# A hybrid diffusion layer on one core: the first stage rebuilt, with array turns over loaded tiles, splits on VectorE, and four jobs moved into it

## The chip, the cores and the metric

The kernel runs on one core of one Trainium2 chip. The metric is the device time of one execution in microseconds (us), lower being better; the figure of record is the median over the runs.

## The reference

One layer of a diffusion backbone over 512 latent tokens `x` (width 1024) with a prefix of 256 context tokens `ctx`, all in float32. A conditioning row `c` gives six modulation vectors of 1024 for the latent tokens (`silu(c) @ w_ada + b_ada`), a vector `c_ctx` gives them for the context:

```
hx = rmsnorm(x, g_pre_mix)   * (1 + scale)     + shift
hc = rmsnorm(ctx, g_pre_mix) * (1 + scale_ctx) + shift_ctx
px, pc = hx @ w_in, hc @ w_in          # cut into the inputs of three branches and three gates
a = HGRN2 recurrence, both directions, 4 heads of 128   (from a state over the context)
b = grouped-query attention over context and latent tokens, q and k normed, rotary
c = Hyena: dwconv3, u = v * x1, long convolution of u with filters, times x0
y = (sum of sigmoid(gate) * (branch @ w_o)) @ w_out
x = x + gate1 * rmsnorm(y);   x = x + gate2 * rmsnorm(ConvFFN(modulate(x)))
```

The Hyena filters come from a small network over 512 positions: three layers `h = sin(freq * (h @ w + b))` of width 64 (33 inputs), and a last matrix.

## The kernel before, in words

**Dense matmuls.** Activations are held transposed, channels on partitions, tokens along the row. Every large matmul is made of three passes of 32-bit operands that are split into a high and a low part: high weights by high activations, high by low, low by high (`passes`, matmul at L251). A split is a ScalarE copy that rounds (L206) and a subtraction that makes the remainder (L209), on VectorE unless the caller names GpSimd. `weights` issues the load of a weight tile into one of three buffers `w_raw` on SP's queue and splits it. A "job" is 8 k tiles x 3 passes = 24 matmuls of 512 columns with one weight tile; `stream` runs jobs in turn and loads `ahead` of them. L254 is the line of transposes.

**The first stage, `begin`.** It loads the tokens (`xT`, eight tiles of 128 x 512) and the first modulation tiles, and adds up the squares of the tokens (L527). A modulation vector isn't a matmul: for each of 128 x 1024 tiles of `w_ada` one VectorE instruction (L462, with its read of the accumulator) multiplies by the row `silu(c)`, which a matmul with ones has spread over all partitions, and sums along the row. `rstd_` makes the reciprocal root mean squares of the tokens: tiny matmuls of the squares with ones, VectorE's mean (L849), GpSimd's power (L850), four diagonal tiles (L853), and matmuls with ones that spread them (`rb`). Then, for each of the eight k tiles: the load of two modulation tiles and of one tile of `w_first` (six weight groups of 128, the heads' q and gate of heads 0 to 2), their split with the remainder on GpSimd, two modulation columns (L462, bias L490, scale L491), x times `rb` (L548), scale and shift on ScalarE, and the split into `hx_h` and `hx_l`. With each tile 18 matmuls run, six groups that stay open in PSUM banks 0 to 5 over all k tiles. At four of the tiles one step of the filter network (`filter_net`, `sin`, L326 to L333) stands between. Behind this the context is normed (`norm`, on GpSimd and VectorE), and six Hyena jobs run (`hy_jobs`, part 2 and 1 of channel tiles 0 to 2), with GpSimd making the weights' remainders. Each job ends in `conv3`: a ScalarE step (L865) and two VectorE steps (L866, L867) of a convolution of three taps. Between the steps of these jobs the context is modulated tile by tile into `hc`.

**The rest, `run`.** A planner (`weave`) walks through twelve streams in one fixed order of preference (the recurrence's mixes, states, outputs, the Hyena convolution, attention, the norms, and the dense jobs as the last) with assumed delays, and so fixes TensorE's order for good; where a stream of higher rank waits, a job fills. The jobs are taken in a list: heads 0 and 1 (two gate jobs and one of values each), two jobs of head 3, two Hyena jobs, head 2, and so on. A gate job has two matmul chains, one of 512 columns for the latent tokens and one of 256 for the context; each is evacuated by two sigmoids on ScalarE (L615, L616). The dense jobs alternate between two PSUM banks (`dbanks`). The other four modulation vectors are made behind numbered jobs (`ADA_AT`): each such job lets `ada_rest` issue one load (L586) and do one column (L462); the tiles of these loads lie in two buffers in turn.

**Engines run in order.** Each engine takes its instructions in the order of the program, and SP issues the loads, in order as well, each when the buffer it fills is free. ScalarE loads a table (ACT_TABLE_LOAD) when the next function is of another set.

## Time and profile before

| | |
|---|---|
| Runs | 1156.64, 1156.71 and 1157.84 us; median 1156.71 |
| Profiled execution | 1156.59 us, span of its trace 1154.8 us |
| TensorE busy | 1082.2 us (94%), 5746 matmuls |
| VectorE, ScalarE, GpSimd busy | 776.0, 500.4, 180.5 us |
| Mean granted clock of TensorE | 0.979 |
| Bytes moved | 119.70 MB, 104 GB/s over the span |
| First 131 us | TensorE 98.90 us busy, VectorE 112.20, GpSimd 48.69, 186 GB/s |
| 131 to 300 us | TensorE 168.83 us of 169 busy |

The trace is that of one execution. Times in it count from the start of its span; the execution lasts 1.8 us longer than the span. A row of the timeline has the start, the duration from the first to the last of the instructions it groups, the engine, the line, the operation, output and inputs by the program's names, shapes and number; in brackets stands the idle time ahead of it with what ended it. "PE" is TensorE, "DVE" VectorE, "ACT" ScalarE, "POOL" GpSimd, "SP" the engine that issues most loads. A row of stretches has for each engine the busy time and the number of instructions, and then the clock granted to TensorE, the share of the time in which the DMA engines were busy, and GB/s.

### The profile page before, as it was taken

Reading aid. Unit: us, or ns where it says so; the run is one execution under the profiler, and the core shown is the slowest. Engines: PE = TensorE matmul, PEld = TensorE weight load, DVE = VectorE, ACT = ScalarE, POOL = GpSimd, SP = SyncE. Lnnn points to the kernel's source line nnn. Section 1 sums busy time; section 2 is a strip of 40 time slices with the busy share of each in tenths; the row PEclk is TensorE's granted clock in tenths of the full one; section 3 lists DMA queues with packets and bytes.
Section 4 is the critical chain, followed back from the end, with each engine's and each line's share of the span. In section 5 each row is a group of like instructions: output and inputs, shape, how many; then the busy total and the mean of one; then the engine's idle time right before and its main releaser. Section 6 shows DMA issues by size and latency. Waiting matters only on the chain.

```text
span 1154.8 us, 14924 instructions
## 1 busy us (share of the span) xinstructions
PE 1082.2 (94%) x5746; PEld 922.5 (80%) x5746; DVE 776.0 (67%) x1265; ACT 500.4 (43%) x799; POOL 180.5 (16%) x179
## 2 busy tenths in 40 slices
PE   4888999999999988999999999889999999999995
PEld 2566799898888876977888878889888888888885
DVE  5998997968874775886667658365786666531124
ACT  4454543334333432665555555345444444332220
POOL 2256212011212022102111100320000000001112
PEclk9989999999998998999999999989999999999998
DMA  9632623513433211420112254111362332223212
GB/s 329 232 94 87 205 92 91 165 55 110 128 101 101 83 55 53 130 94 34 55 56 63 82 167 151 50 37 56 128 200 92 100 120 91 82 69 100 82 51 74
DMA packets 36437, 119.70 MB, mean 104 GB/s; under 512 B 3948, under 2 KB 6188, under 8 KB 36366
## 3 DMA queue, kind: packets, MB, share of 16 engines
q1 hardware_dynamic: 33980, 111.97, 29.9%
q0 software_dynamic: 1152, 4.19, 1.3%
q10 hardware_dynamic: 1234, 2.58, 0.7%
q8 instruction: 45, 0.74, 0.3%
q14 instruction: 26, 0.21, 0.1%
HBM read 116.63 MB, written 2.10 MB: 103 GB/s over the span
## 4 chain that ended last, share of the span: by engine, by line
PE 74%; DVE 14%; ACT 4%; issue 3%; POOL 2%; DMA 2%; ACTq 0%; DVEq 0%; POOLq 0%
PE banks L251 71%; DVE page L209 2%; PE banks L254 2%; DVE page L462 2%; ACT page L206 1%; DVE page L1362 1%; DVE page L1363 1%; DVE hx_l L209 1%; DMA page<-in_w_ada 1%; DMA w_raw<-in_w_in 1%; POOL page L853 1%; DVE wide L774 0%; POOL page L209 0%; DVE page L1071 0%; DVE wide L772 0%
## 5 line engine op out<-in xcount | busy, mean ns | idle before, releaser
L251 PE MATMUL banks<-hx_h,page 128*128 128x512 f32 (+1 forms) x1768 | 564.9, 389 | 16.7 <-ACT hx_h L206 4.5
L251 PEld LDWEIGHTS banks<-hx_h,page 128*128 128x128 f32 x1768 | 333.6, 192 | 85.9 <-issue 8.3
L251 PE MATMUL banks<-page,page 128*128 128x256 f32 (+4 forms) x1991 | 379.9, 323 | 10.5 <-ACT page L1254 5.5
L251 PE MATMUL banks<-hx_l,page 128*128 128x512 f32 (+1 forms) x872 | 338.3, 388 | 2.7 <-DVE hx_l L209 2.7
L251 PEld LDWEIGHTS banks<-page,page 128*128 128x128 f32 (+2 forms) x1991 | 303.2, 192 | 44.7 <-ACT page L1254 5.9
L209 DVE TENSOR_TENSOR page<-w_raw,page 128x1024 fp32r<-128x1024 f32 (+2 forms) x139 | 164.2, 1184 | 154.9 <-ACT page L206 99.7
L206 ACT ACTIVATE page<-w_raw 128x1024 fp32r<-128x1024 f32 (+2 forms) x154 | 155.9, 1016 | 140.0 <-PE banks L251 120.7
L251 PEld LDWEIGHTS banks<-hx_l,page 128*128 128x128 f32 x872 | 167.8, 192 | 32.5 <-DVE hx_l L209 3.6
L251 PE MATMUL banks<-thin,page 128*128 128x512 f32 (+1 forms) x367 | 112.9, 355 | 0.6 <-DVE thin L209 0.6
L251 PEld LDWEIGHTS banks<-thin,page 128*128 128x128 f32 x367 | 67.7, 191 | 9.8 <-DVE thin L209 1.1
L462 DVE SCALAR_TENSOR_TENSOR page<-page,page 128x1024 f32<-128x1024 f32 x52 | 63.4, 1221 | 7.4 <-DMA page<-in_w_ada 5.2
L1352 POOL TENSOR_TENSOR page<-page,thin 128x256 f32<-128x256 f32 x7 | 7.8, 1120 | 326.3 <-ACT thin L1302 326.3
L1172 POOL TENSOR_SCALAR page<-page,page 128x768 f32<-128x768 f32 x32 | 29.2, 914 | 169.7 <-DVE page L1171 166.0
L1170 ACT ACTIVATE page<-banks,page 128x768 f32<-128x768 f32 x32 | 31.7, 991 | 31.8 <-DVE page L1169 29.6
L206 ACT ACTIVATE page<-page 128x512 fp32r<-128x512 f32 (+1 forms) x45 | 24.7, 552 | 43.2 <-DVE page L1455 20.1
L254 PE MATMUL banks<-const,page 128*128 128x128 f32 x254 | 38.0, 275 | 1.1 <-ACT page L1031 1.1
L209 POOL TENSOR_TENSOR page<-w_raw,page 128x768 fp32r<-128x768 f32 (+1 forms) x14 | 32.4, 2312 | 42.0 <-ACT page L206 42.0
L254 PEld LDWEIGHTS banks<-const,page 128*128 128x128 f32 x254 | 31.8, 146 | 8.2 <-ACT page L1031 1.3
L206 ACT ACTIVATE page<-banks 128x512 fp32r<-128x512 f32 x41 | 24.1, 593 | 29.4 <-PE banks L254 29.4
L865 ACT ACTIVATE page<-banks,vec 128x512 f32<-128x512 f32 x40 | 30.5, 766 | 14.1 <-PE banks L251 14.0
L251 PEld LDWEIGHTS banks<-const,page 128*128 128x128 f32 x132 | 20.0, 219 | 17.5 <-DVE page L1407 7.5
L768 ACT ACTIVATE page<-wide 128x512 f32<-128x512 f32 x28 | 19.0, 678 | 34.1 <-DVE wide L774 18.0
(277 smaller groups left out, 1127.9 us busy)
## 6 DMA issues: line engine op xcount, KB each, us to landing
w_raw<-in_w_in SPq DMA_DIRECT2D x58, 512.0 KB, 3.5
w_raw<-in_w_up SPq DMA_DIRECT2D x44, 512.0 KB, 3.5
page<-in_w_ada SPq DMA_DIRECT2D x42, 512.0 KB, 4.4
w_raw<-in_w_down SPq DMA_DIRECT2D x16, 512.0 KB, 3.5
w_raw<-in_w_out SPq DMA_DIRECT2D x8, 512.0 KB, 3.8
w_raw<-in_w_first SPq DMA_DIRECT2D x8, 384.0 KB, 7.3
wide<-in_w_ada SPq DMA_DIRECT2D x6, 512.0 KB, 4.6
w_raw<-in_w_down SPq DMA_DIRECT2D x8, 384.0 KB, 3.1
```

The costliest lines, as they stand in the source:

```text
L206: self.nc.scalar.activation(h, x, AF.Copy, scale=1.0 if scale is None else scale)
L209: e.tensor_tensor(l, x, hf, op=SUB)
L251: self.on_pe(self.nc.tensor.matmul(out, w, x, start=start, stop=stop), max(n, 64) * (1 if x.dtype == F32R else 4))
L254: self.on_pe(self.nc.tensor.transpose(out, x, self.cv(C_ID, 128)), 256)
L462: self.nc.vector.scalar_tensor_tensor(junk, w, 1.0, row, op0=MUL, op1=MUL, accum_out=out)
L768: nc.scalar.activation(km.v(0, [(2 * b, n2), (b, 2), (1, b)]), kq.v(1024, [(2 * b, n2), (b - 1024, 2), (1, b)]), AF.Copy)
L853: (engine or nc.gpsimd).tensor_scalar(dg[:, c * 128:(c + 1) * 128], self.cv(C_ID, 128), ms[:, 4 + c:5 + c], 1.0, op0=MUL, op1=MUL)
L865: nc.scalar.activation(out, ps, AF.Identity, bias=w[:, 3:4], scale=w[:, 1:2])
L1170: nc.scalar.activation(p[:], s, AF.Exp, bias=st[:, 1:2], scale=r, accum_out=st[:, 2:3])
L1172: gp.tensor_scalar(p[:], p[:], st[:, 3:4], 1.0, op0=MUL, op1=MUL)
L1362: e.tensor_tensor(y, y, rs.v(0, [(0, 2), (1, 256)]), op=MUL)
L1363: e.tensor_tensor(r, r, y, op=ADD)
```

## The change

- **Start.** The tokens' loads alternate between SP's queue and ScalarE's; the constants' load comes behind them. Ones that the matmuls need come from a memset. The conditioning row is spread and passed through SiLU ahead of the squares. Behind each square, and over the first two pairs of modulation tiles, `warm` runs matmuls of ones with the loaded tile; nobody reads their bank. The tokens' `rb` comes from a function `shares`, whose diagonal is one instruction.
- **Splits** of `w_first` and of the Hyena weights: VectorE in place of GpSimd.
- **Modulation in three steps** (`modulated`): VectorE multiplies x by scale and `rb`, ScalarE adds the shift and rounds into `hx_h`, VectorE adds the shift and subtracts `hx_h`. The biases of two columns are added by one instruction (`mods_of`, now L494, L495).
- **Filter network folded**: the 512 positions lie as two halves of 256 on partitions 0 and 64, with block-diagonal weights. Its first layer stands ahead of the k tiles, the other two behind the dense jobs of `begin`; the last sine writes both halves into rows of 64.
- **Context later**: its row is made behind the k tiles, its squares after eight steps of the dense jobs, and its `rb` by `shares`; `norm` is gone.
- **Four jobs moved**: the q and gate jobs of head 3 and the two Hyena jobs of channel tile 3 go from the list of `run` into `begin`, which then runs ten dense jobs over five banks in turn. The second part of `ADA_AT` is four numbers lower.

Lines in the changed program stand a little apart: the split's L206 and L209 are L205 and L208, the gate's L615 and L616 are L639 and L640, `conv3` is L889 to L891, and the modulation's remainder is L484.

```diff
-ADA_AT = list(range(1, 28)) + list(range(90, 107, 2))
+ADA_AT = list(range(1, 28)) + list(range(86, 103, 2))
...
-NET = (1, 3, 5, 7)
...
-    def filter_net(self):
+    def filter_net(self, banks):
+
 
         nc, i = self.nc, self.i
-        sm, z = self.A(512), self.A(512)
-        nc.sync.dma_start(sm[:64, :196], i["hy_small"])
-        nc.sync.dma_start(z[:33, :], i["zT"])
-
-        h = None
-        arg, tmp = self.A(512), self.A(512)
+        n = T // 2
+        sm, z = self.A(512), self.A(n)
+        nc.scalar.dma_start(sm[:, :388], i["hy_small"])
+        nc.scalar.dma_start(z[:], i["zT"])
+
+        h, (arg, tmp) = z, (self.A(n) for _ in range(2))
         for l in range(3):
-            yield 9.0
-            ps = self.cbank()
...
+            yield
+            ps = self.bank(banks[l])[:, :n]
+            self.mm(ps, sm[:, 128 * l:128 * l + 128], h[:], True, True)
+            nc.vector.tensor_scalar(arg[:], ps, sm[:, 384 + l:385 + l], sm[:, 387:388], op0=ADD, op1=MUL)
+            self.sin(arg[:], tmp[:])
+            self.free(h)
+            if l < 2:
+                h = self.A(n)
+                nc.scalar.activation(h[:], arg[:], AF.Sin)
+        h = self.A(T)
+        for half in range(2):
+            nc.scalar.activation(h[:64, half * n:half * n + n], arg[64 * half:64 * half + 64, :], AF.Sin)
+        self.free(sm, arg, tmp)
         self.fh = h
...
-    def norm(self, xt, n):
+    def shares(self, ps, n, rb):
 
         nc, v = self.nc, self.nc.vector
...
+        k = n // 128
+        ms, dg = self.A(16), self.A(n)
+        v.tensor_scalar(ms[:, 0:k], ps.v(0, [(2, k)]), 1.0 / D, EPS, op0=MUL, op1=ADD)
+        nc.gpsimd.tensor_tensor(ms[:, 4:4 + k], ms[:, 0:k], self.cv(C_NH, k), op=ALU.pow)
+        v.tensor_tensor(dg.v(0, [(128, k), (1, 128)]), Buf(self.const).v(C_ID, [(0, k), (1, 128)]), ms.v(4, [(1, k), (0, 128)]), op=MUL)
+        for c in range(k):
+            self.mm(rb[:, c * 128:(c + 1) * 128], self.cv(C_ONE, 128), dg[:, c * 128:(c + 1) * 128], True, True)
+        self.free(ms, dg)
+
+    def modulated(self, m, o, ft, x, rb, hl):
+
+        nc, v = self.nc, self.nc.vector
+        n = x.shape[-1]
+        u, (h, l) = self.A(n), hl
+        shift = m[:, o + ft:o + ft + 1]
+        v.scalar_tensor_tensor(u[:, :n], x, m[:, o + 16 + ft:o + 17 + ft], rb, op0=MUL, op1=MUL)
+        self.last_mod = nc.scalar.activation(h, u[:, :n], AF.Identity, bias=shift).ins
+        v.scalar_tensor_tensor(l, u[:, :n], shift, h.bitcast(F32), op0=ADD, op1=SUB)
+        self.free(u)
+
+    def mods_of(self, m, o, ft, w, row, junk=None):
 
         v = self.nc.vector
         for part in range(2):
...
+            c = o + 8 * part + ft
+            self.ada(m[:, c:c + 1], w[part][:], row, w[part][:] if junk is None else junk)
+        p = m.v(o + ft, [(8, 2)])
+        v.tensor_tensor(p, p, Buf(self.vec).v(V_BADA + ft, [(8, 2)]), op=ADD)
+        v.scalar_tensor_tensor(m[:, o + 16 + ft:o + 17 + ft], m[:, o + 8 + ft:o + 9 + ft], 1.0, self.vv(V_G + ft), op0=ADD, op1=MUL)
 
     def begin(self):
 
         nc, i, v = self.nc, self.i, self.nc.vector
...
+        row, ones = self.A(1024), self.A(256)
+        v.memset(ones[:], 1.0)
         xb, cb = [self.A(512) for _ in range(8)], [self.A(512) for _ in range(4)]
         xt = [b[:] for b in xb]
...
         for k, b in enumerate(xb):
-            nc.sync.dma_start(b[:], i["xT"][:, k * 512:(k + 1) * 512])
-        rows = [self.A(1024) for _ in range(2)]
+            (nc.sync, nc.scalar)[k % 2].dma_start(b[:], i["xT"][:, k * 512:(k + 1) * 512])
+        nc.scalar.dma_start(self.const, i["const"])
+        net = self.filter_net((4, 5, 5))
+        next(net)
         self.row = rows[0]
         wada, groups = [], [Buf(self.bank(g)) for g in range(6)]
         def load_ada(ft):
...
+        load_ada(1)
+        for k in range(2):
+            ps = self.bank(k)
+            self.mm(ps, ones[0:1, :128], row[0:1, k * 512:(k + 1) * 512], True, True)
+            nc.scalar.activation(rows[0][:, k * 512:(k + 1) * 512], ps, AF.Silu)
+        self.free(row)
+        junk = self.A(1024)
+
+        def warm(x):
+            self.mm(self.bank(3), ones[:, :128], x, True, True)
         sqs = []
         for k in range(KT):
             sq = self.A(512)
-            last = nc.scalar.activation(sq[:], xt[k], AF.Square).ins
+            nc.scalar.activation(sq[:], xt[k], AF.Square)
+            warm(xt[k])
...
-        rs = self.rstd([sqs[0]], C_ONE, 1.0 / D, engine=v)
+        ps, rb = Buf(self.bank(7)), Buf(self.bank(6))
+        for c in range(4):
+            self.mm(ps[:, 2 * c:2 * c + 2], sqs[0][:, c * 128:(c + 1) * 128], ones[:, :2], c == 0, c == 3)
         self.free(sqs)
-        self.cbanks.remove(6 + self.comp_bank % 2)
-        net = self.filter_net()
+        self.shares(ps, T, rb)
+        for e in range(8):
+            warm(wada[e // 4][e // 2 % 2][:, e % 2 * 512:e % 2 * 512 + 512])
+        next(net)
         for ft in range(KT):
-            if ft:
+            if ft > 1:
                 load_ada(ft)
-            if ft in NET:
-                next(net, None)
-            wh, wl = self.weights(i["w_first"][ft], (6, 128), nc.gpsimd)
-            self.mods_of(m, ft, [b[:] for b in wada[ft]], rows[0][:], junk[:])
-            v.tensor_tensor(xt[ft], xt[ft], rs[:], op=MUL)
-            self.modulated(m, ft, xt[ft], self.hx[ft], "hx")
+            wh, wl = self.weights(i["w_first"][ft], (6, 128))
+            self.mods_of(m, 0, ft, wada[ft], rows[0][:], junk[:])
+            self.modulated(m, 0, ft, xt[ft], rb[:], self.hx[ft])
             for g in range(6):
                 s = slice(g * 128, (g + 1) * 128)
                 self.passes(groups[g][:], wh[:, s], wl[:, s], *self.hx[ft], ft == 0, ft == KT - 1)
             self.done((wh, wl))
+        self.free(xb, junk, ones)
+        rows.append(self.A(1024))
+        nc.sync.dma_start(rows[1][:], i["cond"][1:2, :].to_broadcast([128, D]))
+        nc.scalar.activation(rows[1][:], rows[1][:], AF.Silu)
         for k, b in enumerate(cb):
             nc.sync.dma_start(b[:], i["cT"][:, k * 512:(k + 1) * 512])
-        nc.sync.dma_start(rows[1][:], i["cond"][1:2, :].to_broadcast([128, D]))
-        nc.scalar.activation(rows[1][:], rows[1][:], AF.Silu)
...
+        self.dbanks = [4, 0, 2, 1, 3]
...
+        jobs = [j for c in range(3) for j in self.hy_jobs(c)[:2]] + list(self.hg_jobs(3))[3:] + self.hy_jobs(3)[:2]
+        dense = self.stream(jobs)
+        for _ in range(8):
+            next(dense)
+        sqs = [self.A(512) for _ in cb]
+        for b, sq in zip(cb, sqs):
+            nc.scalar.activation(sq[:], b[:], AF.Square)
+        for k in (1, 2, 3):
+            v.tensor_tensor(sqs[0][:], sqs[0][:], sqs[k][:], op=ADD)
+        for e in range(4):
+            self.mm(ps[:, e % 2 * 2:e % 2 * 2 + 2], sqs[0][:, e * 128:(e + 1) * 128], self.cv(C_ONE, 2), e == 0, e == 3)
+        self.free(sqs)
+        self.shares(ps, TC, rb)
         for ft in range(KT):
-            for _ in range(8):
-                next(hy, None)
-            self.mods_of(mc, ft, [b[:] for b in wada[ft]], rows[1][:])
-            self.modulated(mc, ft, ct[ft], self.hc[ft], "hc")
-        for _ in hy:
+            for _ in range(9):
+                next(dense, None)
+            self.mods_of(m, 24, ft, wada[ft], rows[1][:])
+            self.free(wada[ft])
+            self.modulated(m, 24, ft, ct[ft], rb[:, :TC], self.hc[ft])
+        for _ in dense:
             pass
-        self.free(cb, m, mc, wada, rows[1], self.slots)
+        for _ in net:
+            pass
+        self.free(cb, m, rows[1], self.slots)
         self.slots = []
-        self.cbanks = [2, 3, 4, 5, 6, 7]
+        self.dbanks, self.cbanks = [0, 1], [2, 3, 4, 5, 6, 7]
...
-        hy = self.hy_jobs(3)[:2]
         x0 = [self.hy_jobs(c)[2] for c in range(4)]
         at = list(self.at_jobs())
-        jobs = P[0] + P[1] + P[3][3:] + hy + P[2] + at[:2] + P[3][:3] + at[2:] + x0
+        jobs = P[0] + P[1] + P[2] + at[:2] + P[3][:3] + at[2:] + x0
...
```

On VectorE at the start of the program (L527 and L539 add squares, L208 is the remainder of a weight split, `w_raw` the loaded weights), before:

```order
L527 TENSOR_TENSOR page_133<-page_133,page_141 128x512
L527 TENSOR_TENSOR page_122<-page_122,page_133 128x512
L462 SCALAR_TENSOR_TENSOR page_105,page_149<-page_117,page_115 128x1024
L849 TENSOR_SCALAR page_154<-banks 128x4
L462 SCALAR_TENSOR_TENSOR page_105,page_149<-page_118,page_115 128x1024
L853 TENSOR_SCALAR page_157<-const,page_154 128x128 x4
```

and after:

```order
L539 TENSOR_TENSOR page_152<-page_152,page_159 128x512
L208 TENSOR_TENSOR page_89<-w_raw_70,page_88 128x768
L539 TENSOR_TENSOR page_152<-page_152,page_163 128x512
L494 TENSOR_TENSOR page_93<-page_93,vec 128x2
L208 TENSOR_TENSOR page_91<-w_raw_71,page_90 128x768
L539 TENSOR_TENSOR page_137<-page_137,page_152 128x512
L495 SCALAR_TENSOR_TENSOR page_93<-page_93,vec 128x1
L462 SCALAR_TENSOR_TENSOR page_136,page_93<-page_128,page_107 128x1024
L469 TENSOR_SCALAR page_122<-banks 128x4
L462 SCALAR_TENSOR_TENSOR page_136,page_93<-page_129,page_107 128x1024
L471 TENSOR_TENSOR page_172<-const,page_122 128x512
```

Before, the additions stand ahead of everything else; after, two weight splits stand between the last of them, and one more modulation column ahead of the diagonal.

On ScalarE around the first gate job, the first work of the planner's list (L615 and L616, after L639 and L640, evacuate a gate's bank, 512 columns for the latent tokens and 256 for the context), before:

```order
L615 ACT_TABLE_LOAD
L615 ACTIVATE page_353<-banks 128x512
L616 ACTIVATE page_94<-banks 128x512
L206 ACTIVATE page_1089<-w_raw_71 128x1024
L615 ACTIVATE page_205<-banks 128x256
L616 ACTIVATE page_96<-banks 128x256
```

and after (L367 and L370 are the sines of the filter's second and third layer, L889 the last job's convolution):

```order
L889 ACTIVATE page_428<-banks,vec 128x512
L639 ACT_TABLE_LOAD
L639 ACTIVATE page_93<-banks 128x256
L367 ACT_TABLE_LOAD
L367 ACTIVATE page_119<-page_119 128x256
L640 ACT_TABLE_LOAD
L640 ACTIVATE page_103<-banks 128x256
L205 ACTIVATE page_875<-w_raw_69 128x1024
L370 ACT_TABLE_LOAD
L370 ACTIVATE page_95<-page_119 64x256 x2
L639 ACT_TABLE_LOAD
L639 ACTIVATE page_119<-banks 128x512
```

The order of the two evacuations is reversed, the 512 columns come last, and both sines and three more table loads stand ahead of them.

On VectorE at the same place of the changed program (L362, L330 to L335: bias and argument of a filter layer; L462 into `mods`: columns of `ada_rest`):

```order
L462 SCALAR_TENSOR_TENSOR page_92,mods<-page_92,page_107 128x1024
L333 SCALAR_TENSOR_TENSOR page_119<-page_122,page_119 128x256
L462 SCALAR_TENSOR_TENSOR page_136,mods<-page_136,page_107 128x1024
L335 TENSOR_SCALAR page_119<-page_119 128x256
L462 SCALAR_TENSOR_TENSOR page_92,mods<-page_92,page_107 128x1024
L462 SCALAR_TENSOR_TENSOR page_136,mods<-page_136,page_107 128x1024
L362 TENSOR_SCALAR page_119<-banks,page_118 128x256
L641 SCALAR_TENSOR_TENSOR page_428<-page_93,page_103 128x256
L330 TENSOR_SCALAR page_122<-page_119 128x256
L642 SCALAR_TENSOR_TENSOR page_428<-page_428,page_97,page_93 128x256
L331 TENSOR_SCALAR page_122<-page_122 128x256
L333 SCALAR_TENSOR_TENSOR page_119<-page_122,page_119 128x256
```

The second layer's argument (L335) stands between modulation columns that alternate between two buffers, and two such columns stand ahead of the third layer (L362) behind it. Before, the network was done at this place.

More of the change, by code (lines that the diff above doesn't have):

```diff
@@ L321, in vv, with sin @@
         return self.vec[:p, c0:c0 + n]
-    def sin(self, out, arg, tmp, p):
+    def sin(self, arg, tmp):
         v = self.nc.vector
@@ L507, in begin @@
-        row = junk = self.A(1024)
+        ct = [cb[k // 2][:, k % 2 * 256:k % 2 * 256 + 256] for k in range(KT)]
+        rows, m = [self.A(1024)], self.A(48)
         nc.scalar.dma_start(row[0:1, :], i["cond"][0:1, :])
         for k, b in enumerate(xb):
-            nc.sync.dma_start(b[:], i["xT"][:, k * 512:(k + 1) * 512])
-        rows = [self.A(1024) for _ in range(2)]
+            (nc.sync, nc.scalar)[k % 2].dma_start(b[:], i["xT"][:, k * 512:(k + 1) * 512])
+        nc.scalar.dma_start(self.const, i["const"])
@@ L1650, in constants @@
     z = np.concatenate([t, np.cos(fw), -np.sin(fw)], -1).astype(f32)
+    zT = np.zeros((128, T // 2), f32)
+    zT[:33], zT[64:97] = z[:T // 2].T, z[T // 2:].T
     deltas = np.abs(np.linspace(math.log(1e-2) / 1.5, math.log(1e-2) / 0.3, 512, dtype=f32))
@@ L1661, in constants @@
     rope = np.concatenate([np.tile(co, (4, 1)), np.concatenate([-si, si, -si, si])], 1).astype(f32)
-    return {"const": c, "masks": masks, "fwd": fwd, "inv": inv, "zT": z.T, "decay": decay, "rope": rope}
+    return {"const": c, "masks": masks, "fwd": fwd, "inv": inv, "zT": zT, "decay": decay, "rope": rope}
 def groups(w, cols):
@@ L1710, in layout @@
     a["w_down"] = groups(w_down[0], 128)
-    small = np.zeros((64, 196), np.float32)
-    small[:33, 0:64] = hy_w1[0]
-    small[:, 64:128] = hy_wi[0][0]
-    small[:, 128:192] = hy_wi[0][1]
-    small[:, 192] = hy_b1[0]
-    small[:, 193:195] = hy_bi[0].T
-    small[:, 195] = hy_freq[0]
+    small = np.zeros((128, 388), np.float32)
+    for half in (0, 64):
+        small[half:half + 33, half:half + 64] = hy_w1[0]
+        for l in range(2):
+            small[half:half + 64, 128 + 128 * l + half:192 + 128 * l + half] = hy_wi[0][l]
+        small[half:half + 64, 384] = hy_b1[0]
+        small[half:half + 64, 385:387] = hy_bi[0].T
+        small[half:half + 64, 387] = hy_freq[0]
     a["hy_small"] = small
```

53 lines of the change are left out of this document (3 added, 50 removed).

## The prediction, made before the changed kernel ran

> **What bounds the kernel now.** I read the stretches first: the start, the two parts of the first stage, and the 169 us behind them. Columns are PE, weight loads, DVE, ACT and POOL busy with their counts, then granted clock, DMA share and GB/s.
>
> ```profile
> 0.00:10.00 10.00, 3.77 (x4) 1.15 (x4) 2.68 (x4) 5.06 (x7) 0.19 (x4) 1.00 0.79 258
> 10.00:20.00 10.00, 2.08 (x9) 2.00 (x10) 6.70 (x12) 4.47 (x6) 3.76 (x2) 1.00 1.02 369
> 24.00:72.00 48.00, 41.81 (x150) 30.01 (x150) 46.55 (x83) 22.48 (x35) 17.41 (x8) 0.96 0.57 198
> 72.00:131.00 59.00, 49.38 (x206) 38.61 (x204) 53.55 (x101) 30.30 (x48) 27.32 (x19) 0.91 0.38 118
> 131.00:300.00 169.00, 168.83 (x1098) 152.57 (x1099) 144.99 (x263) 64.60 (x111) 27.34 (x33) 1.00 0.37 120
> ```
>
> From 131 us on TensorE has work all the time (168.83 of 169); before that it has not, and VectorE is the busy one (46.55 of 48, 53.55 of 59). So only the first 131 us can be won, and the place to compare is the start of the second gate job, the first thing TensorE does once it never waits. I read that place, and the speed of TensorE, in the timeline.
>
> ```profile
> 24.15 2.50 PE L251 MATMUL banks<-hx_h,page 128*128 128x512 f32 x5 [2.29 <-ACT hx_h L206]
> 34.34 0.39 PE L251 MATMUL banks<-hx_h,page 128*128 128x512 f32 x1
> 36.16 0.39 PE L251 MATMUL banks<-hx_h,page 128*128 128x512 f32 x1
> 75.04 0.80 PE L251 MATMUL banks<-hx_h,page 128*128 128x512 f32 x1 [2.76 <-DVE page L675]
> 76.06 1.05 PE L251 MATMUL banks<-hx_h,page 128*128 128x512 f32 x2
> 77.34 1.05 PE L251 MATMUL banks<-hx_h,page 128*128 128x512 f32 x2
> 81.18 0.64 PE L251 MATMUL banks<-hx_h,page 128*128 128x512 f32 x2
> 126.49 3.03 PE L251 MATMUL banks<-page,page 128*128 128x256 f32 x24
> 131.03 0.50 PE L251 MATMUL banks<-hx_h,page 128*128 128x512 f32 x1 [1.51 <-ACT page L616]
> ```
>
> Eight steps of one 512-column matmul lie between 34.34 and 36.16: 0.2275 us each. A job of 24 takes 5.46 us. The 24 context matmuls of a gate job take 3.03. After 2.76 us without work the steps are 1.28/3 = 0.427 us, until 81.18: 6.1 us at little more than half speed, a loss of 6.1 x (1 - 0.2275/0.427) = 2.9 us.
>
> VectorE, GpSimd and ScalarE, same view:
>
> ```profile
> 13.57 1.86 PE L251 MATMUL banks<-const,page 128*128 128x2 f32 x8 [4.45 <-DVE page L527]
> 15.39 0.84 ACT L206 ACTIVATE page<-w_raw 128x768 fp32r<-128x768 f32 x1 [0.93 <-DMA w_raw<-in_w_first]
> 15.64 0.16 DVE L849 TENSOR_SCALAR page<-banks 128x4 f32<-128x4 f32 x1
> 15.88 1.99 POOL L850 TENSOR_TENSOR page<-page,const 128x4 f32<-128x4 f32 x1 [15.45 <-DVE page L849]
> 19.78 2.08 PE L251 MATMUL banks<-page,const 128*128 128x128 f32 x8 [4.35 <-DVE page L853]
> 23.46 0.63 ACT L206 ACTIVATE hx_h<-page 128x512 fp32r<-128x512 f32 x1
> 30.77 0.68 DVE L209 TENSOR_TENSOR hx_l<-page,hx_h 128x512 fp32r<-128x512 f32 x1
> 36.84 1.21 DVE L462 SCALAR_TENSOR_TENSOR page<-page,page 128x1024 f32<-128x1024 f32 x1
> 37.91 1.83 POOL L209 TENSOR_TENSOR page<-w_raw,page 128x768 fp32r<-128x768 f32 x1 [3.56 <-ACT page L206]
> 37.99 0.07 DVE L462 DVE_READ_ACCUMULATOR page<-page,page 128x1 f32 x1
> 37.99 2.30 DVE L209 TENSOR_TENSOR hx_l<-page,hx_h 128x512 fp32r<-128x512 f32 x1
> 72.37 0.41 DVE L331 TENSOR_SCALAR page<-page 64x512 f32<-64x512 f32 x1
> 119.37 0.74 DVE L867 SCALAR_TENSOR_TENSOR page<-banks,vec,page 128x511 f32<-128x511 f32 x1
> 120.03 0.15 DVE L490 TENSOR_TENSOR page<-page,vec 128x1 f32<-128x1 f32 x1
> 120.10 1.22 DVE L209 TENSOR_TENSOR page<-w_raw,page 128x1024 fp32r<-128x1024 f32 x1
> 121.23 0.15 DVE L491 SCALAR_TENSOR_TENSOR page<-page,vec 128x1 f32<-128x1 f32 x1
> 128.60 1.28 ACT L615 ACT_TABLE_LOAD   x1
> ```
>
> The same remainder (hx_l) takes 0.68 us alone and 2.30 beside a GpSimd split: while GpSimd runs a split, VectorE stands. Start to start, VectorE needs 1.22 us for a modulation column (36.84 to 37.99, and its 0.07), 1.13 for a 1024-wide split (120.10 to 121.23), 0.66 for a half convolution (119.37 to 120.03), 0.07 for a one-column step. I take 0.88 for a 768-wide split (768/1024 of 1.13, and a little), 0.65 for 512 elements, and half of a 512-wide step for 256.
>
> **The change part by part.** At the second gate job the changed program has done four jobs more (two of head 3, two of Hyena): 4 x 24 x 0.2275 = 21.8 us. If it starts that job at S, and TensorE stays full from there as it does now, the gain is 131.03 + 21.8 - S = 152.8 - S. S has four terms.
>
> *A, to the first dense matmul.* Now 24.15. The sums of squares no longer run first: in VectorE's queue two weight splits stand ahead of their last additions, and the second waits for a transfer that has 5.8 MB queued up to and with it, and about 0.5 MB of the next in flight beside it. By the rows above 6.3 MB have passed at 20 us (258 and 369 GB/s). The x tiles go out from two queues, so the first 10 us should run nearer the rate of the next ten; I take 19.0, bounds 17.5 and 20. Then ScalarE 0.84, split 0.88, last addition 0.65: 21.4. Sums to the scale's first step 2.1 (13.57 to 15.64), 0.15, GpSimd's power 2.0, the diagonal, now one instruction of 512, 0.65: 26.3. Behind it on VectorE stand the filter's first layer (0.4), a modulation column (1.22) and two small ones (0.3); TensorE's 2.08 fits beside them: 28.2. Modulation 0.65, ScalarE 0.63: **A = 29.5** (27.5 to 31.5). The array's turns over loaded tiles lie in this idle time and cost nothing while the second modulation tile has landed by the time of the sums; each turn left over is four passes, 4 x 0.2275 = 0.9 us. The Trainium skill, "DMA: Bandwidth & Descriptors", "Issuing engines are not separate DMA queues", says that several issuing engines save only issue time; by it A would be 20.0 + 10.5 = 30.5 and the time 1 us longer. The 0.79 share of the first 10 us leaves room for either; no run shows it yet.
>
> *B, the eight k tiles.* GpSimd's splits and their blocking are gone, but the splits are now VectorE's. From the first modulation on its queue holds 11 columns (13.4), 6 splits (5.3), 15 modulations and remainders (9.8), the rest of the filter layer (1.4) and 13 small steps (0.9): 30.8, so VectorE still sets the pace: 5.2 us per tile against 18 x 0.2275 = 4.1 of TensorE. It ends at 28.85 + 30.8 = 59.7. The remainder of the tile before the last stands 1.5 us earlier, at 58.2; behind it TensorE has 14 + 18 matmuls, 7.3 us: 65.5. **B = 36.0** (33 to 39).
>
> *C, the ten jobs.* Six Hyena jobs, now without GpSimd, and the four moved ones: 10 x 5.46 = 54.6. Ahead of them the first bank's copy, 0.65. Context sums and broadcast sit inside: about 1.1, and 1.2 of waiting for its scale. VectorE has 16 columns (19.5), 12 splits (13.6), 12 half convolutions (7.9), 16 context steps (5.4) and some 8 us of products, gates and small steps: 54, just less than TensorE. **C = 57.6** (57 to 62): the tenth job ends at 123.1.
>
> *D, from there to the second gate job.* Now 8.5 + 1.5 = 10.0 (first gate job, and the wait before 131.03). In the changed order the evacuation of the first gate job's 512 columns stands on ScalarE behind both later filter layers, and the second gate job needs that bank. Counted from the end of the tenth job: ScalarE's split and the convolution's first step 1.7; VectorE's two half convolutions, product, split, two modulation columns and the second filter layer bring 8.9; the sine waits for it, the next layer's matmul follows at 11.1. But the third layer stands in VectorE's queue behind four modulation columns whose tiles are loaded into two buffers, each load issued only when the column two before it is done.
>
> ```profile
> L586 SPq DMA_DIRECT2D page<-in_w_ada x32: 327/328/384, 102.3 to 850.7; - x32
> DMA to landing us min/median/max: 3.5/4.0/5.1
> ```
>
> The columns end at 7.2, 8.7, then 7.2 + 4.0 + 1.2 = 12.4, 8.7 + 5.2 = 13.9, 17.6, 19.1. Three small steps: 19.8. Two sines of 0.45, the table load 1.28 and two sigmoids of 0.5: **D = 23.2** (21 to 27 by 3.5 and 5.1 per load). TensorE has 9.0 of work in it and stands for 13 us where it stood 1.5. It restarts slow: 2.9 us, as after the 2.76 above (0 to 3.1). The Trainium skill, "TensorE: Matmul & The Clock Gate", "What's actually happening", gives full rate back after one busy window of about 3.4 us; by it the loss would be 1.6 and the time 1.3 us shorter.
>
> S = 29.5 + 36.0 + 57.6 + 23.2 = 146.3, with the slow start 149.2; the gain is 152.8 - 149.2 = 3.6. The profiled execution took 1156.59 us (span 1154.8, 1.8 around it), 0.12 under the median of the runs, so I forecast 1156.6 - 3.6 = **1153.0**.
>
> At nothing: the remaining modulations are drawn at the same jobs as before (four numbers lower, four jobs fewer), behind a TensorE that is full; the folded filter's last sine only moves rows. Heads 1 and 2 now follow each other without the four jobs between; the 144.99 of 169 of VectorE leave 24 us there, against 8 us of VectorE work and 21.8 of TensorE that move out, so I price it at 0, bound 6.
>
> **The rivals.** *The filter's tail costs nothing.* If VectorE comes early to the two layers, or the six loads return in time, D is 10.0 and there is no slow restart: 13.2 + 2.9 us less, 1137. For it: the order says what stands behind what, not how long a load takes, and at the 3.5 us that is the row's least the columns end 1 us earlier. Against: the tenth job's convolution stands ahead, and nothing on VectorE passes it. Chance 0.12.
>
> *Slower: the heads' recurrences come out of their cover.* Each head's mix has seven levels, each a chain VectorE, ScalarE, TensorE, VectorE. Now head 1's mix runs beside gate jobs, which need VectorE themselves, and not beside plain jobs. 14 levels of heads 1 and 2 decide: from 3.6/14 = 0.26 us per level the gain is gone; at 0.6 it is 8.4, 1157.8 + 3 for the layers behind them in Hyena, about 1160. For it: VectorE is 86% busy there. Against: TensorE waits 0.17 in 169 us now. Chance 0.2.
>
> *The start is later still.* Transfers share the same engines; if the second split's tile lands at 23 instead of 19, every term moves by 4: 1157. Chance 0.13.
>
> **How the numbers follow.** The forecast has 0.55, the rivals 0.12, 0.2, 0.13. The bounds of A, B, C and D around it add to about 6 either way if they don't all fall together: 1147 to 1159. I reach to the slow side as far as the second rival and toward the first, but not to it: 1144 to 1162. A measurement can tell about 0.2% (2.3 us) from no change. Most of the forecast's case lies beyond that, some within: faster 0.55, same 0.19, slower 0.26.
>
> **What would show it.** First dense matmul near 29.5; the eight tiles' last near 65; ten jobs done near 123; TensorE idle for some 13 us before a matmul that waits for ScalarE's L640, with VectorE waiting for modulation tiles in that gap, and a slice of lowered clock behind it; then full again to 300 us. No remainder (L484) of over 1 us. I am wrong if that gap is under 5 us, if the ten jobs end 5 us off, or if TensorE falls under 95% between the gap and 290 us.

## The result, and the profile after

The changed kernel takes 1146.84 us (median of 5 runs, 1140.81 to 1148.12), the kernel before 1156.71 (5 runs, 1155.92 to 1158.9): a ratio of 0.9901, 95% interval 0.9872 to 0.993. That is 9.9 us won, where 3.6 was forecast. The profiled execution took 1147.83 us (span 1146.1), 8.76 less than that of before, and its sum is made against that.

The stretches of the changed kernel, cut at the ends of the prediction's four terms; columns as before:

```profile
0.00:10.00 10.00, 5.43 (x6) 1.66 (x6) 0.27 (x1) 1.42 (x2) 0.19 (x4) 1.00 0.80 264
31.53:68.01 36.48, 35.48 (x144) 27.89 (x145) 33.88 (x66) 16.41 (x23) 0.00 (x0) 0.96 0.50 170
68.01:124.70 56.69, 56.11 (x253) 46.32 (x252) 55.58 (x106) 26.25 (x37) 1.71 (x2) 1.00 0.46 147
124.70:149.46 24.76, 9.63 (x54) 8.01 (x52) 16.92 (x37) 12.19 (x15) 0.64 (x1) 0.75 0.54 171
149.46:154.20 4.74, 4.74 (x11) 3.77 (x12) 2.42 (x3) 0.00 (x0) 1.13 (x1) 0.51 0.00 0
154.20:320.00 165.80, 164.11 (x1104) 149.24 (x1102) 134.81 (x241) 66.20 (x117) 29.13 (x38) 1.00 0.25 77
```

The eight k tiles now keep TensorE busy (35.48 of 36.48), the ten jobs as well (56.11 of 56.69, with VectorE at 55.58). Then come 24.76 us with 9.63 of work, and a stretch at a clock of 0.51. TensorE's timeline there and at the start:

```profile
4.57 22.07 PE L250 MATMUL banks<-page,page 128*128 128x512 f32 x46 [4.57 <-DMA page<-in_xT]
28.25 1.16 PE L250 MATMUL banks<-page,const 128*128 128x128 f32 x8 [1.61 <-DVE page L471]
31.53 2.93 PE L250 MATMUL banks<-hx_h,page 128*128 128x512 f32 x6 [2.13 <-ACT hx_h L483]
130.62 3.03 PE L250 MATMUL banks<-page,page 128*128 128x256 f32 x24
135.94 0.67 PE L250 MATMUL banks<-page,page 128*128 128x256 f32 x2 [2.29 <-ACT page L367]
149.46 0.80 PE L250 MATMUL banks<-hx_h,page 128*128 128x512 f32 x1 [12.84 <-ACT page L640]
```

The second gate job waits 12.84 us for L640, the evacuation of the first gate job's 512 columns. What that stands behind, on VectorE and then on ScalarE:

```profile
130.67 1.22 DVE L462 SCALAR_TENSOR_TENSOR page<-page,page 128x1024 f32<-128x1024 f32 x1
132.15 1.22 DVE L462 SCALAR_TENSOR_TENSOR page<-page,page 128x1024 f32<-128x1024 f32 x1
136.76 1.23 DVE L462 SCALAR_TENSOR_TENSOR page<-page,page 128x1024 f32<-128x1024 f32 x1 [3.17 <-DMA page<-in_w_ada]
138.27 1.22 DVE L462 SCALAR_TENSOR_TENSOR page<-page,page 128x1024 f32<-128x1024 f32 x1 [0.28 <-DMA page<-in_w_ada]
139.42 0.54 DVE L362 TENSOR_SCALAR page<-banks,page 128x256 f32<-128x256 f32 x1
...
144.23 1.22 DVE L462 SCALAR_TENSOR_TENSOR page<-page,page 128x1024 f32<-128x1024 f32 x1 [1.05 <-DMA page<-in_w_ada]
...
145.83 0.29 DVE L335 TENSOR_SCALAR page<-page 128x256 f32<-128x256 f32 x1
```

```profile
146.16 0.84 ACT L370 ACTIVATE page<-page 64x256 f32<-64x256 f32 x2 [6.42 <-DVE page L335]
147.02 1.28 ACT L639 ACT_TABLE_LOAD   x1
148.32 0.60 ACT L639 ACTIVATE page<-banks 128x512 f32<-128x512 f32 x1
148.81 0.59 ACT L640 ACTIVATE page<-banks 128x512 f32<-128x512 f32 x1
```

That is the predicted tail: four columns, then the third layer (L362), its steps between two more columns, the sines, a table and the evacuation.

The other difference lies where none was forecast, near 440 us. First before, then after:

```profile
442.07 2.88 PE L251 MATMUL banks<-page,page 128*128 128x512 f32 x12
450.47 5.49 PE L251 MATMUL banks<-page,page 128*128 128x512 f32 x12 [5.52 <-ACT page L1254]
```

```profile
436.88 5.60 PE L250 MATMUL banks<-page,page 128*128 128x512 f32 x24
444.76 0.50 PE L250 MATMUL banks<-hx_h,page 128*128 128x512 f32 x1 [2.28 <-DVE page L1293]
```

Before, a job of a merge (two chains of 12 matmuls, each into a bank of its own) is cut in two: its second half waits 5.52 us for a bank's evacuation and then runs at half speed (12 matmuls in 5.49 us, against 2.88 for the first 12). ScalarE comes to that evacuation (L1254) only at 449.82, behind copies that waited 4.05 us for GpSimd and 3.00 for VectorE. After, the evacuation of the gate job just ahead (L1278) has no such copies in front of it and starts at 437.13; the 24 matmuls run in one piece, and the wait behind them is 2.28 us.

### The profile page after: what moved, and what is told of

It reads as the page before. It is cut to its first block, busy times and chain, and to the rows that moved or that the text cites. A ratio compares the mean times of both kernels' runs of the same rounds, so it can differ in the third digit from the quotient of the medians.

```text
span 1146.1 us, 14945 instructions
## 1 busy us (share of the span) xinstructions
PE 1084.1 (95%) x5778; PEld 921.6 (80%) x5778; DVE 767.2 (67%) x1270; ACT 492.3 (43%) x781; POOL 133.3 (12%) x152
## 4 chain that ended last, share of the span: by engine, by line
PE 78%; DVE 10%; DMA 4%; issue 3%; ACT 3%; POOL 2%; ACTq 0%; POOLq 0%; DVEq 0%
PE banks L250 76%; DMA page<-in_w_ada 2%; PE banks L253 2%; DVE page L208 2%; DVE page L462 2%; DVE page L1386 1%; DVE page L1387 1%; ACT page L205 1%; DMA const<-in_const 1%; ACT page L1194 0%; DVE page L1095 0%; DMA page<-in_xT 0%; DMA w_raw<-in_w_up 0%; POOL page L874 0%; DMA w_raw<-in_w_first 0%
## 5 line engine op out<-in xcount | busy, mean ns | idle before, releaser
L250 PE MATMUL banks<-page,page 128*128 128x256 f32 (+2 forms) x1940 | 385.3, 328 | 13.0 <-DMA page<-in_xT 4.6
L250 PEld LDWEIGHTS banks<-page,page 128*128 128x128 f32 x1940 | 297.2, 192 | 57.2 <-issue 18.4
L208 DVE TENSOR_TENSOR page<-w_raw,page 128x1024 fp32r<-128x1024 f32 (+2 forms) x156 | 181.5, 1166 | 155.0 <-ACT page L205 98.9
L205 ACT ACTIVATE page<-w_raw 128x1024 fp32r<-128x1024 f32 (+2 forms) x157 | 157.9, 1010 | 141.2 <-PE banks L250 116.6
L250 PE MATMUL banks<-thin,page 128*128 128x512 f32 (+1 forms) x472 | 134.8, 349 | 1.9 <-ACT thin L205 1.3
L250 PEld LDWEIGHTS banks<-thin,page 128*128 128x128 f32 x472 | 84.4, 193 | 12.6 <-ACT thin L205 1.7
L462 DVE SCALAR_TENSOR_TENSOR page<-page,page 128x1024 f32<-128x1024 f32 x54 | 65.9, 1222 | 24.5 <-DMA page<-in_w_ada 12.7
L1376 POOL TENSOR_TENSOR page<-page,page 128x256 f32<-128x256 f32 x21 | 18.4, 888 | 397.9 <-ACT page L1326 397.9
L205 ACT ACTIVATE page<-page 128x512 fp32r<-128x512 f32 (+1 forms) x35 | 20.6, 593 | 55.9 <-DVE page L1479 23.6
L889 ACT ACTIVATE page<-banks,vec 128x512 f32<-128x512 f32 x44 | 33.6, 766 | 9.4 <-PE banks L250 9.4
L253 PEld LDWEIGHTS banks<-const,page 128*128 128x128 f32 x254 | 31.5, 144 | 7.2
L890 DVE SCALAR_TENSOR_TENSOR page<-banks,vec,page 128x511 f32<-128x511 f32 x44 | 32.7, 745 | 5.7 <-ACT page L889 5.7
L205 ACT ACTIVATE page<-banks 128x512 fp32r<-128x512 f32 x43 | 25.3, 593 | 25.9 <-PE banks L253 25.9
L208 DVE TENSOR_TENSOR page<-banks,page 128x512 fp32r<-128x512 f32 x35 | 24.0, 687 | 14.8 <-ACT page L205 14.7
```

Source lines behind the costliest of these rows:

```text
L205: self.nc.scalar.activation(h, x, AF.Copy, scale=1.0 if scale is None else scale)
L208: e.tensor_tensor(l, x, hf, op=SUB)
L250: self.on_pe(self.nc.tensor.matmul(out, w, x, start=start, stop=stop), max(n, 64) * (1 if x.dtype == F32R else 4))
L253: self.on_pe(self.nc.tensor.transpose(out, x, self.cv(C_ID, 128)), 256)
L462: self.nc.vector.scalar_tensor_tensor(junk, w, 1.0, row, op0=MUL, op1=MUL, accum_out=out)
L889: nc.scalar.activation(out, ps, AF.Identity, bias=w[:, 3:4], scale=w[:, 1:2])
```

## Experiments

Each kernel was compared with the kernel before on its own chip; the medians of before were 1157.03, 1155.51 and 1155.38 us in the three groups. Runs of one kernel spread by 4 to 15 us. The gap of "24.6" in the expectations is the 24.76 above, counted from the end of the tenth job's last matmul (124.86) and not from the start of the next one.

**The filter's two later layers between the dense jobs** (group 1).

```diff
                 next(dense, None)
+            if ft in (1, 4):
+                next(net, None)
             self.mods_of(m, 24, ft, wada[ft], rows[1][:])
```

> The changed kernel with the filter network's second and third layer run between the ten dense jobs. Theory (the layers behind the jobs hold ScalarE's evacuation of the first gate job, and so the second gate job): the stretch from the end of the tenth job to the second gate job falls from 24.6 us to about 9.5 (24 x 0.2275 + 3.03 of the gate job and 1), the slow steps behind it (2.1 us lost) go, and the two layers cost VectorE some 5 us in a stretch that has 1 us to spare, 2 to 4 of it seen: 1147.8 - 15.1 - 2.1 + 3 = about 1134. Rival (the modulation columns and their loads hold the gate, whatever the filter does): 1143 to 1148, the gap stays over 8 us.

Measured 1130.65 us (4 runs, 1130.14 to 1134.09), ratio 0.9773 (0.9716 to 0.983). The second gate job waits 1.06 us:

```profile
131.01 3.03 PE L250 MATMUL banks<-page,page 128*128 128x256 f32 x24
135.10 0.50 PE L250 MATMUL banks<-hx_h,page 128*128 128x512 f32 x1 [1.06 <-ACT page L642]
```

So the layers behind the jobs did hold the gate; between them they hide. The gate starts 14.4 us earlier, and no slow steps follow.

**The four jobs back in the planner's list** (group 1): the changed kernel with `P[0] + P[1] + P[3][3:] + hy + P[2]` and the numbers of `ADA_AT` of before.

> The changed kernel with the four moved jobs back in the planner's list, where the kernel before had them; TensorE's order behind the first gate job is then word for word that of before. Theory (the 7.3 us won behind the second gate job come from the other order that the planner makes once the four jobs are out of its list): they are gone, the stop of 5.5 us near 440 us and its slow steps are back, and only the start's gain of 1.3 is left: about 1155. Rival (they come from the first stage, which leaves VectorE and the loads further ahead): about 1148, the stop near 440 us stays under 3 us.

Measured 1149.86 us (10 runs), 0.9934 (0.9909 to 0.9958): the rival's time, but the stop is back as the theory has it (and ScalarE's waits of 4.06 and 3.01 us ahead of that evacuation with it):

```profile
101.97 0.59 PE L250 MATMUL banks<-page,page 128*128 128x256 f32 x2
102.21 0.59 PE L250 MATMUL banks<-hx_h,page 128*128 128x512 f32 x1
112.97 1.22 PE L250 MATMUL banks<-hx_h,page 128*128 128x512 f32 x2 [9.94 <-DVE page L208]
...
433.11 2.88 PE L250 MATMUL banks<-page,page 128*128 128x512 f32 x12
441.51 2.93 PE L250 MATMUL banks<-page,page 128*128 128x512 f32 x6 [5.53 <-ACT page L1278]
```

My number had carried the changed kernel's gap over. Here the gap is another one: with six jobs TensorE is done at 102 us, while VectorE still makes the context's columns, and the first gate job waits 9.94 us for its weight split behind them.

**No array turns over loaded tiles** (group 1): both calls of `warm` taken out, which leaves out only matmuls that nobody reads.

> The changed kernel without the array's turns over the loaded tiles. Theory (turns left over hold the sums of squares back by 2.3 us, and 2.7 us of slow steps follow them all the same): the first dense matmul comes 2 us earlier, near 29.5, and slow steps last at most as long as the 6.1 us seen in the kernel before, 1.6 us more lost than now: within 1 us of the changed kernel, 1147. Rival (the turns keep the array fast): the start isn't earlier, and the slow steps cost 1.6 to 3 us more: 1150.

Measured 1151.65 us (10 runs), 0.9961 (0.9932 to 0.9991). The first dense matmul came at 32.72, not earlier. Without the turns the scheduler also puts the filter's first layer ahead of the additions on VectorE, where it starts only at 16.82, behind a matmul that waits for the network's input, so the run doesn't separate the two. The run without turns over modulation tiles, below, does it better.

**Four buffers for the first modulation columns** (group 1).

```diff
-            raw = [self.A(1024) for _ in range(2)]
+            raw = [self.A(1024) for _ in range(2 if part else 4)]
```

> The changed kernel with four buffers in place of two for the first eight modulation columns behind the dense jobs; TensorE's order is the same. Theory (the columns ahead of the filter's third layer wait for loads that are issued only when a buffer is free): VectorE's waits of 3.2, 0.3 and 1.1 us for those tiles go, and the gap before the second gate job falls from 24.6 to about 20: 1143. Rival (the filter's own chain of steps sets it): the gap stays within 1 us, 1147.8.

Measured 1152.51 us (10 runs), 0.995 (0.9919 to 0.998), and the gap is as long: TensorE waits 12.56 us. But the edit doesn't do what it was made for. It allocates four buffers, while the lines behind it still load into `raw[j % 2]` and read `raw[(j - 1) % 2]`: two of the four are used. The trace shows it too, since each load still goes out 0.02 to 0.03 us after the read that ends a column:

```profile
133.49 0.09 DVE L462 DVE_READ_ACCUMULATOR page<-page,page 128x1 f32 x1
133.60 0.33 SPq L610 DMA_DIRECT2D page<-in_w_ada  x1
134.97 0.08 DVE L462 DVE_READ_ACCUMULATOR page<-page,page 128x1 f32 x1
135.08 0.33 SPq L610 DMA_DIRECT2D page<-in_w_ada  x1
```

So the run decides nothing between the theory and its rival: what four buffers would do stays open. Why it is slower than the changed kernel (0.995 against 0.990) isn't known either.

**The changed kernel again** (group 2).

> The changed kernel once more, beside the next three on the same chip, as their yardstick: 1147 against 1157 of before, a ratio near 0.990, whichever theory holds.

Measured 1145.06 us (4 runs), 0.9899 (0.9868 to 0.993); second gate job at 149.26.

**Splits back on GpSimd** (group 2): `nc.gpsimd` for `w_first` and for the Hyena weights.

> The changed kernel with the remainders of w_first and of the Hyena weights back on GpSimd. Theory (a GpSimd split blocks VectorE, so that the remainder beside it takes 2.3 us in place of 0.7; and it is slow itself): the eight k tiles take over 40 us instead of 36.5, the six Hyena jobs come near the 7.5 us each of before instead of 5.5, the second gate job starts 8 to 16 us later: 1155 to 1163. Rival (VectorE sets the pace either way, and what is taken from it comes back): within 3 us of the changed kernel.

Measured 1155.27 us (10 runs), 1.0001 (0.9975 to 1.0028): 10 us slower than the changed kernel beside it, although the later start of the gate leaves the filter's tail less to do:

```profile
156.75 0.80 PE L250 MATMUL banks<-hx_h,page 128*128 128x512 f32 x1 [6.24 <-ACT page L640]
```

The gate starts 7.5 us later (156.75 against 149.26), just under the 8 of the theory. The eight k tiles take 39.2 us (36.5 in the changed kernel, over 40 expected), the six Hyena jobs some 45 (35). Two splits on GpSimd and what VectorE does beside them:

```profile
38.39 1.85 POOL L208 TENSOR_TENSOR page<-w_raw,page 128x768 fp32r<-128x768 f32 x1 [10.75 <-ACT page L205]
38.91 1.88 DVE L484 SCALAR_TENSOR_TENSOR hx_l<-page,page,hx_h 128x512 fp32r<-128x512 f32 x1 [1.53 <-ACT hx_h L483]
46.50 2.56 POOL L208 TENSOR_TENSOR page<-w_raw,page 128x768 fp32r<-128x768 f32 x1 [2.18 <-ACT page L205]
47.28 0.73 DVE L482 SCALAR_TENSOR_TENSOR page<-page,page,banks 128x512 f32<-128x512 f32 x1
```

The remainder (L484) takes 1.88 us where it takes 0.74 alone, as the theory says. But not all of VectorE stands while GpSimd runs a split, as the prediction had it: a modulation that also reads a PSUM bank (L482) takes 0.73 beside the next one. The profiled execution is the fastest of the ten, 1148.11 us, so it doesn't show all of the 10 us. Of the parts that were undone one at a time, this one costs the most.

**Only the four jobs moved** (group 2): the kernel before with the change's job lists and the four lower numbers of `ADA_AT`.

> The kernel before with only the four jobs moved into the first stage; TensorE's order behind the first gate job is then word for word that of the changed kernel. Theory (the order alone removes most of the stop near 440 us and its slow steps): the stop is 2.4 us there instead of 5.5, some 5 to 7 us are won behind the second gate job, and the first stage gives 2 to 4 us back, since two of the four jobs run at the 7.5 us of a Hyena job with GpSimd: 1152 to 1156. Rival (the stop depends on how far ahead VectorE is): the stop stays over 5 us, 1158 to 1161.

Measured 1153.14 us (10 runs), 0.9964 (0.9934 to 0.9994). Near 450 us it has the changed kernel's order and wait:

```profile
444.73 5.60 PE L251 MATMUL banks<-page,page 128*128 128x512 f32 x24
452.60 0.50 PE L251 MATMUL banks<-hx_h,page 128*128 128x512 f32 x1 [2.28 <-DVE page L1269]
```

Its second gate job starts at 157.84, which is 5.0 later than before, with the 21.8 us of moved work taken off; from there to the same matmul near 750 us it needs 590.3 + 21.8 = 612.1 us where before needs 619.6. In these two profiles the order alone wins 7.5 us, and the medians agree: 2.4 us are won in all, with 5.0 given away ahead of the second gate job. The size is rough, since profiles with one order differ over this stretch. With the moved work counted in, it takes 609.7 to 615.0 us (611.9 on average) in the four runs that have the filter's layers between the dense jobs and the four jobs in the first stage, and 616.9, 616.0 and 619.6 (617.5 on average) in the two runs that put the four jobs back and in the kernel before. That makes the order worth some 5 to 8 us.

**Modulation columns five jobs later** (group 2): `ADA_AT = list(range(6, 33)) + ...`.

> The changed kernel with the first part of ADA_AT five numbers later, so that no modulation column stands ahead of the filter's third layer; TensorE's order is the same. Theory (the columns and the loads that they wait for hold that layer): from the second layer's matmul it takes 2.8 us of small steps and a split, two sines, a table load and two sigmoids; the gap of 24.6 falls to about 18 and the time to 1141. Rival (the filter's own chain of steps and table loads sets it): the gap stays over 22 us, 1147.

Measured 1150.16 us (10 runs), 0.9957 (0.994 to 0.9974). The gate's wait falls from 12.84 to 7.13 us:

```profile
130.98 3.80 PE L250 MATMUL banks<-page,page 128*128 128x256 f32 x26
141.92 0.80 PE L250 MATMUL banks<-hx_h,page 128*128 128x512 f32 x1 [7.13 <-ACT page L640]
```

So the columns and their loads held the third layer, as predicted: the second gate job starts 7.3 us earlier than the yardstick's. But the time got worse: between the second gate job and the same matmul near 747 us this run needs 604.7 us, against 591.5 of the yardstick. The 27 columns now lie beside other jobs. VectorE waits 21.0 us in the whole run for tiles of such columns, 12.6 in the yardstick, and the longest stop of TensorE there is 4.3 us in place of 2.3 (both for VectorE's L1293). What each stop costs was not taken apart.

**The first experiment again, and three variants of it** (group 3).

> The changed kernel with the filter network's later layers between the dense jobs, once more, as the yardstick of the next three on the same chip: about 1131 beside 1156 of before, a ratio of 0.977.

Measured 1130.6 us (6 runs), 0.9794 (0.9759 to 0.9829).

> The same with three turns over modulation tiles in place of eight. Theory (the five last turns, 0.86 us each, keep TensorE from the sums of squares for 2.4 us after they are ready): the sums come 2.4 us earlier, the first dense matmul near 29, the whole 1 to 2.4 us less than the yardstick. Rival (the loads of the weights hold the first tile, or TensorE starts slower): within 0.5 us of it.

Measured 1131.63 us (6 runs), 0.9806 (0.9766 to 0.9846).

> The yardstick without any turn over modulation tiles; the turns over the tokens stay. Theory (these turns buy nothing): as with three turns, the first dense matmul near 29 and 1 to 2.4 us less than the yardstick. Rival (they keep the granted clock up): the sums come as early, but the slow steps behind the first dense matmul last 4 us or more in place of 2.7, and the time is that of the yardstick or up to 1 us above.

Measured 1132.34 us (6 runs), 0.9801 (0.9767 to 0.9834). With three and no turns over modulation tiles the first dense matmul starts at 29.93 and 29.09 instead of 30.93, but the second gate job at 136.14 and 135.59 instead of 135.94. What the earlier start wins is gone by then, since VectorE sets the pace of the k tiles, and neither run is faster, though both theories said so: 1.0 and 1.7 us more than the yardstick, which lies within the intervals. In the run without them the first steps are slow for at least 6 us; but so they are in the yardstick's second run, and in its first for about half of that time. The rows are the stretches of 6.07 us from the first dense matmul in the first run, the second run and the variant without turns, with the clock in the third column from the end:

```profile
31.43:37.50 6.07, 6.07 (x20) 4.91 (x21) 6.07 (x14) 1.06 (x2) 0.00 (x0) 0.73 0.29 115
```

```profile
30.93:37.00 6.07, 6.07 (x14) 4.79 (x15) 6.07 (x14) 0.72 (x1) 0.00 (x0) 0.50 0.36 144
```

```profile
29.09:35.16 6.07, 6.07 (x14) 4.79 (x15) 5.36 (x13) 0.00 (x0) 0.00 (x0) 0.50 0.62 250
```

The turns over modulation tiles neither cost nor buy anything that these runs can tell. Whether the turns over the tokens do was not tried by itself.

> The yardstick with the four moved jobs back in the planner's list, TensorE's order behind the first gate job that of before. With the gap gone from both, this shows what the planner's order is worth. Theory (the order without the four jobs wins the 7.2 us behind the second gate job): 6 to 8 us above the yardstick, 1137 to 1139, with a stop of 5.5 us and slow steps near 430 us. Rival (the order is worth little, as the 1149.9 of the changed kernel with the jobs back suggests): within 3 us of the yardstick.

Measured 1148.43 us (12 runs), 0.9944 (0.9925 to 0.9963): 17.8 us above the yardstick, where the theory said 6 to 8 and the rival 3. Both forgot what the four jobs cover:

```profile
103.69 0.59 PE L250 MATMUL banks<-hx_h,page 128*128 128x512 f32 x1
116.55 0.80 PE L250 MATMUL banks<-hx_h,page 128*128 128x512 f32 x1 [12.04 <-DVE page L208]
```

```profile
112.59 1.22 DVE L462 SCALAR_TENSOR_TENSOR wide<-wide,page 128x1024 f32<-128x1024 f32 x1
115.27 1.23 DVE L208 TENSOR_TENSOR page<-w_raw,page 128x1024 fp32r<-128x1024 f32 x1
```

With six jobs TensorE runs dry at 104 us, and the first gate job's split (L208) stands behind the context's columns and modulations on VectorE. With ten, the same VectorE work lies beside 21.8 us more of matmuls. The four kernels together, each as its ratio to before:

| | filter's layers behind the jobs | between the jobs |
|---|---|---|
| four jobs in the planner's list | 0.9934 | 0.9944 |
| four jobs in the first stage | 0.990 | 0.979 |

From the upper left cell, each step alone moves 0.3% at most, which lies within the intervals; both together give 1.4%, since either one alone leaves the other's gap, and the gaps lie at the same place. The start of the second gate job shows it: with 21.8 us added where the four jobs still have to come, it is 146.1 and 148.9 in the upper row, 149.5 and 135.9 in the lower. The last cell, 1130.6 us, beats both kernels of this case. The folded network, the modulation in three steps and the tokens' two queues were not undone one at a time.

## Why the prediction was right or wrong, point by point

The direction and the range were right, the size was not: 3.6 us forecast, 9.9 measured (8.76 in the profiled execution). Term by term:

- **A, 29.5 forecast, 31.53 measured** (its upper bound was 31.5). The last addition ended at 21.9, where 21.4 was forecast. Then the sums waited for turns of the array that were left over; that was named, but priced at nothing:

```profile
25.28 0.16 DVE L469 TENSOR_SCALAR page<-banks 128x4 f32<-128x4 f32 x1 [2.18 <-PE banks L250]
```

  From the last addition to L469 it took 3.4 us in place of 2.1. The variants without those turns start earlier, but don't end earlier, so this miss cost nothing that was measured. The tokens' two queues didn't raise the rate of the first 10 us either: 264 GB/s against 258. That is what the Trainium skill, "DMA: Bandwidth & Descriptors", "Issuing engines are not separate DMA queues", says. The second weight tile came as early as forecast all the same (its copy ended at 19.74, 19.84 forecast), by luck: the next 10 us ran at 404 GB/s where the forecast had 369.
- **B, 36.0 forecast, 36.5 measured**, and **C, 57.6 forecast, 56.7 measured** (its lower bound was 57). VectorE's sums held. The remainder `hx_l` no longer has a slow case:

```profile
L484 DVE SCALAR_TENSOR_TENSOR hx_l<-page,page,hx_h x8: 743/747/751, 32.4 to 61.4; 128x512 fp32r<-128x512 f32 x8
```

  What C didn't say is that the four jobs are what covers VectorE's 55.58 us; without them the first gate job waits (9.94 and 12.04 us in the two runs that put them back).
- **D, 23.2 forecast (its terms as they stand add up to 23.0), 24.76 measured.** The order of columns, layers and evacuations was right, and the four columns ended 14.7 us after the tenth job (13.9 forecast). That the filter's layers behind the jobs hold the gate was shown by the run that moves them, and the columns' part by the run that moves those. The reason that I gave for the columns' pace, two buffers, is read from the trace and was not tested: a column's read ends at 131.90, and the load of the tile after the next goes out right behind it.

```profile
131.93 0.33 SPq L610 DMA_DIRECT2D page<-in_w_ada  x1
```

  The term that was too small is the load: from this issue to its column at 136.76 it took 4.8 us, where 4.0 was forecast, and two rounds of such loads follow each other.
- **Slow steps, 2.9 forecast.** The stretch of 4.74 us at a clock of 0.51 loses 4.74 x (1 - 0.2275/0.427) = 2.2. The Trainium skill's rule ("TensorE: Matmul & The Clock Gate", "What's actually happening") would make it 1.6, an estimate from its window of about 3.4 us; it also says that the count varies from run to run, and it does here, below.

So the second gate job starts at 149.46 (146.3 forecast), and 131.03 + 21.84 - 149.46 - 2.2 = 1.2 us are won there, not 3.6. **The step that failed** is the one "at nothing": that TensorE, full from 131 us on, would have nothing to win or lose behind it, with a bound of 6. From the second gate job to the same matmul near 750 us (the first behind a wait of 4.14 us that all these profiles have) the kernel before needs 619.55 us; the changed one 592.57, and with the moved work 614.4. That is 5.1 less, with the 2.2 of slow steps in it: 7.3 us won by a new order of TensorE's work. Most of it is the stop near 440 us (5.52 to 2.28, and half speed behind it in this profile). The run with only the jobs moved shows it without the rest of the change: 7.5, or some 5 to 8 by all profiles. My reading of 131 to 300 us (168.83 of 169 busy) was right, but the planner's list changed for all that comes after, and the stops beyond 300 us, which the trace of before shows, were not in the sum. So that a win clear of the noise was measured is luck for the most part: the four terms and the slow steps, as measured, give 1.2 us, less than the 2.3 that the prediction calls a change one can tell.

Of the rivals, the first (a tail that costs nothing) didn't happen; the run that moves the tail between the jobs comes to it, and 1137 less the 7.3 us of the new order is 1129.7, where 1130.65 was measured. The second, recurrences that come out of their cover, didn't: behind the slow steps TensorE has 164.11 of 165.80 us of work. (Its price was added up wrong: 8.4 us lost from 1153.0 is 1161.4, not 1157.8.) The third, a start 4 us later by the second split's tile, didn't: the ScalarE copies of both splits ran from 17.91 to 19.74.

## What to carry to other kernels

Work that is taken out of a planner's list changes the order of everything behind it: list the stops of the whole trace, not only those of the stage that is rebuilt, and price the ones that the new order can touch. Where two waits end at the same place, to remove one shows almost nothing (0.3% at most here) and both show 1.4%, so try such steps together before one is given up. Read in the trace whether an experiment's edit took hold, here whether the loads go out earlier, before you read its time. And filler for TensorE belongs where VectorE has a serial backlog; what ends that stage must not stand in the same queues as the next stage's evacuation.

## What was not expected of the hardware

How long TensorE stays at half speed after a stop differs between executions of one program. Behind the same wait of 2.28 us near 440 us the profile of the changed kernel has full clock, and that of its second run has not (stretches of 13 us around it):

```profile
439.00:452.00 13.00, 10.72 (x54) 8.78 (x53) 12.13 (x25) 4.16 (x7) 4.40 (x6) 1.00 0.20 62
```

```profile
437.00:450.00 13.00, 10.72 (x45) 8.55 (x44) 11.95 (x24) 3.71 (x6) 3.81 (x5) 0.87 0.20 62
```

The clock is 1.00 in the one and 0.87 in the other, and 54 matmuls against 45 were started. That such stretches come and go would explain a part of the spread of 4 to 15 us between runs, and the times on record fit it: among the runs of the kernel before, the longer ones have the lower mean granted clock (a correlation of -0.64, -0.69 and -0.75 in the three groups; in the third the fastest, 1150.98 us, has 0.986 and the slowest, 1161.26, has 0.974). No run changes the clock alone, so what sets these stretches stays open.
